# Gate and up biases over 128 rows, down biases in one product at the end

## Chip, core and metric

The kernel runs on one core of one Trainium2 chip. The metric is the device time of one execution in microseconds (us), the median of several runs.

## The reference

A network of two parts works on 512 tokens of width D = 1024 in float32: a first block with a mixed attention and a mixture of experts, then two layers of a second block. The change touches the mixture of experts alone, whose core is:

```
logits = h @ w_router + b_router            # [512, 32]
topv, idx = lax.top_k(logits, 4)
gates = softmax(topv)
# for each expert e and its tokens x:
gu = x @ w_gate_up[e] + b_gate_up[e]        # 1024 -> 2 * 1024
gate = minimum(gu[:, :1024], 7)
up = clip(gu[:, 1024:], -7, 7)
act = (up + 1) * (gate * sigmoid(1.702 * gate))
y = act @ w_down[e] + b_down[e]             # 1024 -> 1024
out[token] += y * gate_of_token
```

and its result is added to the residual x.

## The kernel before

**Accuracy.** A product is near float32 because each operand is held as a value rounded to float32r and the remainder. `split` makes them: ACT writes the rounded tile (`whi`, L50), DVE the remainder (`wlo`, L51). `mm3` then issues three products per tile of weights, L61 with `wlo`, L62 and L63 with `whi`.

**One expert.** Its tokens stand in 96 slots. The weights come in 12 tiles [128, 4, 512] of 1 MB, eight for gate and up and four for down, each loaded by SP into one of eight raw buffers (`fetch`, L85), split by ACT and DVE into four buffers each of `whi` and `wlo`, and used by four groups of three products with 512 columns: 144 products in all. `prep` transposes the gathered rows (L864) and splits them (`exh`, `exl`). `gate_up(e, h)` takes one half of the features: products into two banks G, then the activation with ACT L881 and L882 and DVE L885 to L888, transposed (L891) and split into `ath` and `atl`. `down(e, h)` multiplies a half of the activations into the two banks Y, opened at h = 0; after h = 1 ACT copies the banks, scaled with the gate, into `y` (L912, two buffers), and POOL adds the rows in DRAM by an indirect DMA (`scatter`, L980).

**Biases.** `add_bias` (L846) opens every bank: one product (L848) whose weights are one column of `esel`, broadcast over the 96 slots, over 64 rows, and whose moving operand is 64 rows of the tile `bias`: 32 experts rounded, and 32 remainders. Rows 0 to 63 hold chunks 0 to 2 of 512 columns, rows 64 to 127 chunks 3 to 5; chunks 0 to 3 are gate and up, 4 and 5 down. That is six products per expert, 192 in all, and the tile is made once in `moe_setup` (L810, L812).

**Slots.** `place(e)` finds an expert's tokens and gates: POOL compares (L763), PE multiplies with the one-hot tile (L774 for tokens, L779 for gates), DVE copies (L775, L781, L782). `gather` (L786) fetches the rows. These run up to three experts ahead.

**Order.** The loop over 32 experts issues gate_up(e, 0), prep(e+1), gather(e+2), place(e+3), down(e-1, 1), gate_up(e, 1), down(e, 0). A scheduler in the framework decides how these interleave on each engine; each engine then runs its own list in order. The last expert's result isn't scattered: `yh` and `yl` stay on chip and are added to the loaded sums `xr` in `last(i)` for each of four token tiles, by products with the one-hot tile `pt` (L974) and a DVE addition (L975).

Of the kernel before, what the change touches and what calls it, by code (L numbers as in the profile page):

```python
# [28 lines left out]
# slots of an expert's list in the main path  # L29
NS = 96  # L30
# weight tiles of the experts that are loaded ahead of the router
# [7 lines left out]
class Kern:  # L39
# [6 lines left out]
    def split(self, hi, lo, src, scale=None, eng=None):  # L46
        """hi = src rounded to float32r, lo = src - hi (exact)."""
# [8 lines left out]
    def mm3(self, out, pairs, start=True, stop=True):  # L56
        """out += sum over pairs ((ah, al), (bh, bl)) of a.T @ b in float32 accuracy."""
# [7 lines left out]
    def rstd(self, pool, ss, n, scale, name):  # L65
        """1 / sqrt(ss * scale + EPS): a first value from the exponent's bits and two Newton steps,
        their constants set for the smallest largest error (5e-7)."""
# [21 lines left out]
    def weight(self, src, nk, ncol, pools=None, q=None, parts=1, plan=()):  # L89
        """src: AP [nk*128, ncol] in DRAM. Returns per k tile (hi, lo) APs [128, ncol].  # L90
        plan: for the first chunks, the pools, what the split is to come behind, and the engine of the remainders."""
# [4 lines left out]
        for k0 in range(0, nk, q):  # L96
# [10 lines left out]
            if early:  # L107
                # behind the router's work on each engine
# [15 lines left out]
    def bcast(self, ap, n):  # L124
        """DRAM vector [n] on all partitions."""
        return bass.AP(tensor=ap.tensor, offset=ap.offset, ap=[[0, 128], [1, n]])

    def norm_T(self, i, x, gain, xh, xl, pool, keep=None):
        """Tile i of x [128, D], token-major -> x * rstd * gain, transposed and split."""
# [18 lines left out]
    def setup(self, ctx):  # L148
# [17 lines left out]
        # reversal of the rows  # L166
        rev = self.rev = c.tile([128, 128], F32R, name="rev")
        # diagonal tiles of the second block: a query's own chunk and the earlier ones are open
# [4 lines left out]
    def bias_tables(self, pool):  # L173
        """Bias tables of the banded attention, reversed and extended, over the scale of the scores, split:
        R[m] = 8 * tab[min(639 - m, 256)]"""
# [16 lines left out]
    def probs(self, banks, nh, nk, scale, m, s, normal=False):  # L192
        """banks: scores in psum, [128, nh, nk * 128] each. Leaves the maxima in m and the sums of the exponentials
        in s ([128, heads]); returns per pair of heads and key tile the exponentials, over their sums if normal,
        transposed: (hi, lo) rhs [128, 2 heads, 128]."""
# [34 lines left out]
    def values(self, vs, pr, dst):  # L230
        """Sum over key tiles of values.T @ probs for a pair of heads -> dst [128 (head, dim), 128], whole or (hi, lo)."""
# [10 lines left out]
    def rope_tables(self, pool, cosap, sinap, gain, nrot, name):  # L242
        """A = C * gain, B = Sg * gain with its halves swapped; cos/sin given for the first nrot dims."""
# [18 lines left out]
    def headnorm(self, ps, nh, A, B, nrot, out, i):  # L262
        """ps: psum [128, nh*64] -> per-head rmsnorm and rotation, into out [128, nh, 64]."""
# [3 lines left out]
        # copied, so that the bank is free early  # L267
# [29 lines left out]
    def block1(self):  # L297
# [37 lines left out]
        # fillers after each query tile of the groups and of the dense branch  # L335
# [3 lines left out]
        def bank():  # L339
            """A psum bank of either pool, in turn."""  # L340
            turn[0] += 1
            pool, tag = (self.psS, "S") if turn[0] % 2 else (self.psM, "M")
            return pool.tile([128, 512], F32, name=tag, tag=tag)

        def filler(n=1):
            """Feature tiles of the gates, as tanh(z / 2) = 2 sigmoid(z) - 1, kept in DRAM until the merge."""
# [16 lines left out]
        # masks over key tiles (earlier, own, later): 0 where allowed, NEG elsewhere;  # L363
        # it[p, c] = c - p, key - query = c - p + 128 * rel
# [18 lines left out]
        # keys, transposed and zero-padded: [pair, head of the pair, key]  # L383
# [34 lines left out]
        def scores(qh, ql, p, v, s, j0, j1, mk):  # L418
            """Scores of head s of query pair p, key pair v over key tiles j0..j1."""
# [8 lines left out]
        def scores_b(qh, ql, p, s):  # L428
            """The same for the dense branch; both halves of the partitions hold the keys."""
# [1083 lines left out]
```

## Time and profile before

| | us |
|---|---|
| median of three runs | 3157.68 |
| the three runs | 3156.82, 3157.68, 3165.53 |
| span of the profiled execution | 3154.3 |
| TensorE busy in the span | 3020.5 |
| VectorE busy | 2233.5 |
| ScalarE busy | 1712.6 |

The span runs from the first to the last instruction of one profiled execution. The experts take about 668 to 1936 us of it. Busy times are sums over stages with different limits, so the parts of the experts' stage are read apart, and within them the starts of single instructions. A row of a timeline is: start, duration, engine, line, operation, output<-inputs, shapes, count, and in brackets how long the engine was idle before it and what it waited for. PEld is TensorE's weight load.

### The profile page before, as it was taken

Reading aid. Unit: us, or ns where it says so; the run is one execution under the profiler, and the core shown is the slowest. Engines: PE = TensorE matmul, PEld = TensorE weight load, DVE = VectorE, ACT = ScalarE, POOL = GpSimd, SP = SyncE. Lnnn points to the kernel's source line nnn. Section 1 sums busy time; section 2 is a strip of 40 time slices with the busy share of each in tenths; the row PEclk is TensorE's granted clock in tenths of the full one; section 3 lists DMA queues with packets and bytes.
Section 4 is the critical chain, followed back from the end, with each engine's and each line's share of the span. In section 5 each row is a group of like instructions: output and inputs, shape, how many; then the busy total and the mean of one; then the engine's idle time right before and its main releaser. Section 6 shows DMA issues by size and latency. Waiting matters only on the chain. (4 is left out here: it accounts for less than half of the span.)

```text
span 3154.3 us, 40478 instructions
## 1 busy us (share of the span) xinstructions
PE 3020.5 (96%) x14662; PEld 2327.0 (74%) x14662; DVE 2233.5 (71%) x3715; ACT 1712.6 (54%) x2535; POOL 629.4 (20%) x438
## 2 busy tenths in 40 slices
PE   8999899979999999999999998999999979999998
PEld 6898777766666666666666665878887868888876
DVE  7766587668888988888888987644455585545564
ACT  4645554336776777777777774434444234444432
POOL 1000011033324444444444002111101010111000
PEclk9999999979999999999999998999999989999999
DMA  5122232569999999999999995433435433334362
GB/s 160 61 62 68 88 105 77 181 228 321 350 347 328 338 344 343 343 346 344 343 340 350 344 346 155 128 112 104 122 111 191 150 104 118 113 114 116 102 235 91
DMA packets 407761, 648.48 MB, mean 206 GB/s; under 512 B 23028, under 2 KB 150532, under 8 KB 407556
## 3 DMA queue, kind: packets, MB, share of 16 engines
q1 hardware_dynamic: 387808, 585.73, 55.6%
q0 software_dynamic: 19168, 58.00, 6.1%
q8 instruction: 118, 1.93, 0.3%
q10 hardware_dynamic: 576, 2.10, 0.2%
q14 instruction: 91, 0.71, 0.1%
HBM read 596.16 MB, written 53.79 MB: 206 GB/s over the span
## 5 line engine op out<-in xcount | busy, mean ns | idle before, releaser
L51 DVE TENSOR_TENSOR wlo<-raw,whi 128x2048 fp32r<-128x2048 f32 (+3 forms) x636 | 1157.7, 1831 | 318.6 <-ACT whi L50 314.3
L50 ACT ACTIVATE whi<-raw 128x2048 fp32r<-128x2048 f32 (+3 forms) x646 | 973.2, 1531 | 211.0 <-PE M L63 104.1
L61 PE MATMUL G<-wlo,exh 128*96 128x512 f32 x1024 | 412.8, 403 | 1.8 <-DVE wlo L51 1.8
L63 PE MATMUL G<-whi,exh 128*96 128x512 f32 x1024 | 404.0, 394 | 0.0
L62 PE MATMUL G<-whi,exl 128*96 128x512 f32 x1024 | 403.8, 394 | 0.0
L763 POOL TENSOR_SCALAR poh<-i,rk 128x96 fp32r<-128x96 f32 x124 | 314.4, 2545 | 94.1 <-PE T L779 94.0
L61 PE MATMUL F<-xl,whi 128*128 128x512 f32 x768 | 311.3, 405 | 14.5 <-DVE fl L1199 7.0
L62 PE MATMUL F<-xh,wlo 128*128 128x512 f32 x768 | 304.5, 396 | 1.8 <-DVE wlo L51 1.8
L63 PE MATMUL F<-xh,whi 128*128 128x512 f32 x768 | 304.6, 397 | 0.0
L61 PE MATMUL M<-wlo,xh 128*128 128x512 f32 (+2 forms) x736 | 277.5, 379 | 7.0 <-DVE wlo L51 2.0
L62 PE MATMUL M<-whi,xl 128*128 128x512 f32 (+2 forms) x736 | 276.9, 377 | 0.7 <-DVE xl L51 0.7
L63 PE MATMUL M<-whi,xh 128*128 128x512 f32 (+2 forms) x736 | 273.3, 373 | 0.0
L61 PEld LDWEIGHTS G<-wlo,exh 128*96 128x96 f32 x1024 | 165.5, 162 | 81.2 <-issue 18.2
L63 PEld LDWEIGHTS G<-whi,exh 128*96 128x96 f32 x1024 | 165.5, 162 | 70.4
L62 PEld LDWEIGHTS G<-whi,exl 128*96 128x96 f32 x1024 | 165.9, 162 | 64.2 <-issue 1.2
L61 PE MATMUL Y<-wlo,ath 128*96 128x512 f32 x512 | 210.2, 411 | 2.6 <-POOL wlo L51 1.9
L62 PE MATMUL Y<-whi,atl 128*96 128x512 f32 x512 | 202.1, 395 | 0.0
L63 PE MATMUL Y<-whi,ath 128*96 128x512 f32 x512 | 201.6, 394 | 0.0
L61 PEld LDWEIGHTS F<-xl,whi 128*128 128x128 f32 x768 | 145.3, 189 | 53.4 <-DVE fl L1199 11.2
L61 PEld LDWEIGHTS M<-wlo,xh 128*128 128x128 f32 x736 | 164.7, 224 | 26.3 <-ACT kk L269 4.4
L62 PEld LDWEIGHTS M<-whi,xl 128*128 128x128 f32 x736 | 164.8, 224 | 15.5 <-DVE xl L51 1.4
L63 PEld LDWEIGHTS M<-whi,xh 128*128 128x128 f32 x736 | 164.6, 224 | 14.2 <-issue 0.2
(480 smaller groups left out, 5413.7 us busy)
## 6 DMA issues: line engine op xcount, KB each, us to landing
raw<-in_w_gate_up SPq DMA_DIRECT2D x256, 1024.0 KB, 6.4
raw<-in_w_down SPq DMA_DIRECT2D x124, 1024.0 KB, 7.1
raw<-in_w_in SPq DMA_DIRECT2D x154, 512.0 KB, 3.9
GZ<-fl POOLq DMA_DIRECT2D x80, 256.0 KB, 2.3
raw<-in_w_out SPq DMA_DIRECT2D x24, 512.0 KB, 4.0
raw<-in_w_branch SPq DMA_DIRECT2D x24, 512.0 KB, 4.4
gt<-GZ SPq DMA_DIRECT2D x48, 256.0 KB, 3.1
raw<-in_w_in SPq DMA_DIRECT2D x32, 256.0 KB, 2.9
```

The source lines that it names most:

```text
L50: self.last_act = nc.scalar.activation(hi, src, AF.Copy)
L51: self.last_dve = (eng or nc.vector).tensor_sub(lo, src, f(hi))
L61: nc.tensor.matmul(out, lhsT=ah, rhs=bl, start=start and i == 0, stop=False)
L62: nc.tensor.matmul(out, lhsT=al, rhs=bh, start=False, stop=False)
L63: self.last_mm = nc.tensor.matmul(out, lhsT=ah, rhs=bh, start=False, stop=stop and i == n - 1)
L763: eng.tensor_scalar(oh[:, i], self.i128[:, :NS], self.rk[:, i, e:e + 1], None, op0=ALU.is_equal)
```

## The change

1. `bias` shrinks from [128, 1536] to [128, 1024] and holds only gate and up: rows 0 to 63 chunks 0 and 1, rows 64 to 127 chunks 2 and 3. `esel` becomes [128, 2, 32] with zeros where the other half's rows are, so `add_bias` multiplies all 128 rows.
2. `down` adds no bias; its first product opens the bank. `y` has one buffer, not two.
3. `gates_T`, called once at expert 28, loads b_down three times into 96 rows (a raw buffer), rounds it (`bdn`: rounded, rounded, remainder), copies the gates of all tokens as 96 columns (rounded, remainder, rounded), and transposes them into `gT` [96, 512].
4. `last` opens each bank with a product of `gT` and `bdn`, that is the sum over experts of gate times bias, for all experts at once.
5. The branch for lists over 96 slots (not taken in the trace) drops its addition of b_down. Comments and docstrings are removed, and the lines behind are shifted (L912 becomes L910, L974 becomes L996, L980 becomes L1002).

```diff
-        n = 3 * FF // 2
-        bias = self.bias = mc.tile([128, n], F32R, name="bias")
-        bt = self.mraw.tile([128, 2048], F32, name="bt", tag="raw")[:, :n]
+        bias = self.bias = mc.tile([128, FF], F32R, name="bias")
+        bt = self.mraw.tile([128, 2048], F32, name="bt", tag="raw")[:, :FF]
         for r in (0, 32):
-            nc.sync.dma_start(bt[r:r + 32], a["b_gate_up"][:, :n])
-            nc.sync.dma_start(bt[64 + r:96 + r, :FF // 2], a["b_gate_up"][:, n:])
-            nc.sync.dma_start(bt[64 + r:96 + r, FF // 2:], a["b_down"])
+            nc.sync.dma_start(bt[r:r + 32], a["b_gate_up"][:, :FF])
+            nc.sync.dma_start(bt[64 + r:96 + r], a["b_gate_up"][:, FF:])
...
-        esel = self.esel = mc.tile([128, 32], F32R, name="esel")
+        esel = self.esel = mc.tile([128, 2, 32], F32R, name="esel")
+        nc.gpsimd.memset(f(esel), 0.0)
         for r in range(0, 128, 32):
-            nc.vector.tensor_copy(esel[r:r + 32], self.ident[r:r + 32, r:r + 32])
+            nc.vector.tensor_copy(esel[r:r + 32, r // 64], self.ident[r:r + 32, r:r + 32])
...
         def add_bias(ps, e, c):
-            r = slice(c // 3 * 64, c // 3 * 64 + 64)
-            nc.tensor.matmul(ps, lhsT=esel[r, e:e + 1].to_broadcast([64, NS]), rhs=bias[r, c % 3 * 512:c % 3 * 512 + 512],
-                             start=True, stop=False)
+            nc.tensor.matmul(ps, lhsT=esel[:, c // 2, e:e + 1].to_broadcast([128, NS]),
+                             rhs=bias[:, c % 2 * 512:c % 2 * 512 + 512], start=True, stop=False)
...
-                if h == 0:
-                    add_bias(yp[e][c], e, 4 + c)
-                self.mm3(yp[e][c], [((th[:, k], tl[:, k]), W[k]) for k in range(4)], start=False, stop=h == 1)
+                self.mm3(yp[e][c], [((th[:, k], tl[:, k]), W[k]) for k in range(4)], start=h == 0, stop=h == 1)
             if h == 1 and e < E - 1:
-                y = mp.tile([NS, D], F32, name="y")
+                y = mp.tile([NS, D], F32, name="y", bufs=1)
...
+        gT, bdn = lp.tile([96, S], F32R, name="gT"), lp.tile([96, D], F32R, name="bdn")
+
+        def gates_T():
+            raw = self.mraw.tile([128, 2048], F32, name="bt", tag="raw")
+            bt = raw[:96, :D]
+            for r in (0, 32, 64):
+                nc.sync.dma_start(bt[r:r + 32], a["b_down"])
+            nc.scalar.activation(bdn, bt, AF.Copy)
+            nc.vector.tensor_sub(bdn[64:], bt[64:], f(bdn)[64:])
+            g = raw[:, D:D + NT * 96].rearrange("p (t a e) -> p t a e", t=NT, a=3)
+            for n, c in enumerate((0, 1, 0)):
+                nc.gpsimd.tensor_copy(g[:, :, n], f(self.VG)[:, :, :, c])
+            p = psT.tile([128, 512], F32, name="T", tag="T")[:96]
+            for i in range(NT):
+                nc.tensor.transpose(p[:, i * 128:i * 128 + 128], g[:, i].rearrange("p a e -> p (a e)"), self.ident)
+            nc.scalar.activation(gT, p, AF.Copy)
...
+            if e == E - 4:
+                gates_T()
...
                 ps = self.mbank()
+                ts = slice(i * 128, i * 128 + 128)
+
+                nc.tensor.matmul(ps, lhsT=gT[:, ts], rhs=bdn[:, cs], start=True, stop=False)
                 for n, y in enumerate((yl, yh)):
-                    nc.tensor.matmul(ps, lhsT=pt[:, i * 128:i * 128 + 128], rhs=y[c], start=n == 0, stop=n == 1)
+                    nc.tensor.matmul(ps, lhsT=pt[:, ts], rhs=y[c], start=False, stop=n == 1)
                 nc.vector.tensor_add(xs[i][:, cs], xs[i][:, cs], ps)
```

TensorE (PE), a late expert, around the transposes of the next expert's rows (T from `xg`) and the slot product L774. Before:

```order
L62 MATMUL G<-whi,exl 96x512
L63 MATMUL G<-whi,exh 96x512
L864 MATMUL T<-ident,xg_6279 128x96 x4
L774 MATMUL T<-V,poh 96x2 x4
L848 MATMUL Y<-bias,esel 96x512
L61 MATMUL G<-wlo,exh 96x512
L62 MATMUL G<-whi,exl 96x512
```

After:

```order
L62 MATMUL G<-whi,exl 96x512
L63 MATMUL G<-whi,exh 96x512
L864 MATMUL T<-ident,xg_6280 128x96 x4
L774 MATMUL T<-V,poh 96x2 x4
L61 MATMUL G<-wlo,exh 96x512
L62 MATMUL G<-whi,exl 96x512
L63 MATMUL G<-whi,exh 96x512
```

The product that opened a bank Y is gone from this place, and the dense products of G close up.

VectorE (DVE), a late expert, around the gate copy L781, which waits for PE's L779, and the remainders L51 of weight tiles. Before:

```order
L51 TENSOR_TENSOR wlo<-raw,whi 128x2048 x2
L775 TENSOR_SCALAR gi<-T,spare 96x1
L51 TENSOR_TENSOR exl<-T,exh 128x384
L51 TENSOR_TENSOR wlo<-raw,whi 128x2048
L886 TENSOR_SCALAR gm<-G 96x512
L781 COPY g_12077<-T 96x2
L887 SCALAR_TENSOR_TENSOR sg<-sg,gm 96x512
L782 TENSOR_TENSOR gate<-g_12077 96x1
L51 TENSOR_TENSOR wlo<-raw,whi 128x2048
L885 TENSOR_SCALAR up<-G 96x512
L51 TENSOR_TENSOR wlo<-raw,whi 128x2048
```

After:

```order
L51 TENSOR_TENSOR wlo<-raw,whi 128x2048
L775 TENSOR_SCALAR gi<-T,spare 96x1
L51 TENSOR_TENSOR wlo<-raw,whi 128x2048
L886 TENSOR_SCALAR gm<-G 96x512
L51 TENSOR_TENSOR exl<-T,exh 128x384
L781 COPY g_12351<-T 96x2
L887 SCALAR_TENSOR_TENSOR sg<-sg,gm 96x512
L51 TENSOR_TENSOR wlo<-raw,whi 128x2048
L782 TENSOR_TENSOR gate<-g_12351 96x1
L885 TENSOR_SCALAR up<-G 96x512
L51 TENSOR_TENSOR wlo<-raw,whi 128x2048
```

L782 now stands behind a remainder, one of the remainders ahead of `gi` (L775) is gone from its pair, and `exl` comes between `gm` and the gate copy.

ScalarE (ACT), one expert near the end of the loop, after the change: the copy of `gates_T` (L926) in its surroundings.

```order
L53 ACTIVATE ath<-T 128x384
L50 ACTIVATE whi<-raw 128x2048 x2
L881 ACTIVATE sg<-G,c_6301 96x512
L926 ACTIVATE bdn<-bt 96x1024
L882 ACTIVATE sg<-sg,c_6301 96x512
L50 ACTIVATE whi<-raw 128x2048 x3
L910 ACTIVATE y<-Y,gate 96x512
L50 ACTIVATE whi<-raw 128x2048
```

The copy of b_down has come between the two steps of an activation, L881 and L882.

## Rows read from the trace of the kernel before

**Rows 1.** The page: span of the profiled execution.

```profile
span 3154.3 us, 40478 instructions
```

**Rows 2.** Stretches: us; busy of PE, PEld, DVE, ACT, POOL; PEclk; DMA share; GB/s.

```profile
736.00:966.00 230.00, 230.00 (x1051) 153.75 (x1050) 203.03 (x164) 167.89 (x132) 67.32 (x37) 1.00 1.00 347
1004.00:1892.00 888.00, 887.91 (x3991) 591.90 (x3990) 788.14 (x625) 637.43 (x506) 318.76 (x121) 1.00 1.00 344
```

**Rows 3.** Timeline of PE around one bias product, 936 to 938 us.

```profile
936.07 0.39 PE L62 MATMUL Y<-whi,atl 128*96 128x512 f32 x1
936.30 0.39 PE L63 MATMUL Y<-whi,ath 128*96 128x512 f32 x1
936.62 0.46 PE L848 MATMUL G<-bias,esel 64*96 64x512 f32 x1
937.01 0.47 PE L61 MATMUL Y<-wlo,ath 128*96 128x512 f32 x1
937.32 0.39 PE L62 MATMUL Y<-whi,atl 128*96 128x512 f32 x1
```

**Rows 4.** Timeline of PE around two bias products that coincide.

```profile
904.25 0.39 PE L63 MATMUL G<-whi,exh 128*96 128x512 f32 x1
904.57 0.47 PE L848 MATMUL Y<-bias,esel 64*96 64x512 f32 x1
904.57 0.47 PE L848 MATMUL G<-bias,esel 64*96 64x512 f32 x1
...
905.29 0.39 PE L62 MATMUL G<-whi,exl 128*96 128x512 f32 x1
```

**Rows 5.** Timeline of PE's weight loads around one bias product.

```profile
1907.16 0.15 PEld L848 LDWEIGHTS Y<-bias,esel 64*96 64x96 f32 x1 [0.38 <-issue]
1907.56 0.16 PEld L61 LDWEIGHTS G<-wlo,exh 128*96 128x96 f32 x1 [0.24 <-issue]
1907.64 0.16 PEld L62 LDWEIGHTS G<-whi,exl 128*96 128x96 f32 x1
```

**Rows 6.** Tile bias, by form: duration ns min/median/max, first and last start us.

```profile
L848 PE MATMUL G<-bias,esel x128: 463/470/739, 668.6 to 1885.5; 64*96 64x512 f32 x128
...
L848 PE MATMUL Y<-bias,esel x64: 463/470/738, 689.3 to 1907.2; 64*96 64x512 f32 x64
```

**Rows 7.** The scatter, L980, in 780:950 and 1400:1565 us: duration ns min/median/max.

```profile
L980 POOL DMA_INDIRECT X<-y,gi x5: 1922/1952/1958, 788.4 to 941.0; - x5
...
L980 POOL DMA_INDIRECT X<-y,gi x5: 2265/2292/2295, 1405.1 to 1559.6; - x5
...
DMA to landing us min/median/max: 8.6/8.8/9.9
```

**Rows 8.** Timelines of PE and then DVE, 1491 to 1495 us.

```profile
1491.19 0.42 PE L779 MATMUL T<-VG,poh 128*96 128x2 f32 x4
...
1494.79 0.47 PE L61 MATMUL Y<-wlo,ath 128*96 128x512 f32 x1
...
1491.65 0.15 DVE L781 COPY g<-T 96x2 f32<-96x2 f32 x1 [1.42 <-PE T L779]
1491.73 0.69 DVE L887 SCALAR_TENSOR_TENSOR sg<-sg,gm 96x512 f32<-96x512 f32 x1
...
1492.41 2.28 DVE L51 TENSOR_TENSOR wlo<-raw,whi 128x2048 fp32r<-128x2048 f32 x1
```

**Rows 9.** SP's longest wait, 900 to 1300 us; and one stretch, columns as above.

```profile
SPq L85 <- DVE wlo L51: 314.6, 112, 4.6
...
1420.00:1430.00 10.00, 10.00 (x46) 6.77 (x45) 9.15 (x7) 4.34 (x5) 7.10 (x4) 1.00 1.05 388
```

**Rows 10.** Timeline of the additions behind the experts, 1937 to 1940 us.

```profile
1937.14 0.63 PE L974 MATMUL M<-yl,pt 96*128 96x512 f32 x1
...
1937.57 0.63 PE L974 MATMUL M<-yh,pt 96*128 96x512 f32 x1
...
1939.08 1.06 ACT L133 ACTIVATE xn<-xr 128x1024 f32<-128x1024 f32 x1 [9.60 <-DVE xr L975]
```

More of the change, by code (lines that the diff above doesn't have):

```diff
@@ L1070, in overflow @@
                                 rows(ps, aT, a["w_down"], c * 512)
-                                biased(y[:, c * 512:c * 512 + 512], ps, a["b_down"], c * 512)
-                            nc.vector.tensor_scalar(y, y, gate, None, op0=ALU.mult)
+                                nc.vector.tensor_scalar(y[:, c * 512:c * 512 + 512], ps, gate, None, op0=ALU.mult)
                             self.scatter(y, gi[:, 0:1])
```

## The prediction

> **What bounds the kernel now.** I read the profile in this order: the span, the table of engines by stretch, then the timeline of TensorE (PE) around the products that the change touches, and last the other engines' rows at the one place where PE is closely followed. The span is 3154.3 us [rows 1], the three timed runs have a median of 3157.68 us, so that a run is the span and 3.4 us around it; the sum below is made against the span and added to the median. In both stretches of the experts' stage that are shown, PE is busy in all of the time at full granted clock, DVE in 88 to 89% and ACT in 72 to 73% [rows 2]. There an instruction that PE no longer needs shortens the program, as long as the weight tiles still come in time. The reader should not stop at "PE busy": a busy PE can still run at a poor pitch. So look at the starts: two dense products start 0.23 us apart [rows 3]; I use 0.231, since 144 of them make 33.3 us of an expert. Around a bias product of 64 rows this breaks: product to bias 0.32, bias to next product 0.39, and that one to the one after it 0.31 [rows 3]. From 936.30 to 937.32 us it takes 1.02 us where two pitches are 0.46, so **one bias product costs 0.56 us**, not 0.231. The weight load shows why: it starts late around this product, with PE's loader idle for 0.38 and then 0.24 us on nothing but issue [rows 5]; for the dense product behind it there is none. Two bias products on different halves of the partitions start at the same time, and the pair costs 1.04 less 0.46, 0.58 us [rows 4].
>
> The program has 192 of them, 128 for gate and up and 64 for down [rows 6]. An expert is one scatter: five lie 152.6 us from first to last early, 38.15 each, and 154.5 us late, 38.6 each [rows 7]. In the early pattern one pair of the six products coincides (five costs), later none does (six). The check of this reading: 33.3 + 6 x 0.56 = 36.6, which leaves 2.0 us for the 24 small transposes and slot products of an expert, 0.08 each; with five costs 38.1 comes out, as measured. So the whole period is explained by PE.
>
> **The change part by part.** *Gate and up biases over 128 rows.* Their product becomes like a dense one in rows, columns and type. No row shows one of 128 rows with a broadcast operand: the bounds are 0.231 us (a dense product) and 0.56 (what it is now). I take 0.231, because what sets the 64-row product apart from its neighbours in the rows is its height alone: weights and columns have the same sizes and types.
>
> *Down biases.* 64 products go. *Both together*, per expert: early 5 x 0.56 - 4 x 0.231 = 1.88 us, for 230/38.15 = 6.0 experts, 11.3 us. Late 6 x 0.56 - 0.92 = 2.44 us for (1892 - 966)/38.6 = 24.0 experts, 58.6 us. I count nothing for the first two experts, where PE waits for its inputs.
>
> A rule on this very product stands in the Trainium skill. Its page TensorE: Matmul & The Clock Gate, section "Why this matters for your kernels", says that a single product over 32 rows takes as long as one over 128, and that products on distinct row groups run at the same time. The second half speaks against the change, which gives up the pair that coincides; the trace agrees with it (0.58 us for two), but that is still more than two dense pitches. The trace contradicts its first half: 0.56 us against 0.23.
>
> *What is late next.* With 1.9 to 2.4 us less per expert on PE, the weight tiles must come sooner. The closest follower: PE's gate product L779 at 1491.19 releases DVE's copy L781 at 1491.65, behind which L887 (1491.73) and the remainder of a weight tile (1492.41, 2.28 us long) are queued; PE's first Y product starts 1494.79, 0.10 us after that tile is done [rows 8]. From L779 to Y the chain is 3.50 us and PE's window 3.60. In the changed order the bias product in this window costs 0.33 less and the window is 3.35 where L779 keeps its place: PE waits 0.15 us. The changed order alternates two patterns and one has more products in the window, but the pull on all other tiles grows too. I take twice the worked figure, 0.3 us per expert, 7.2 in the late 24, nothing early; bounds 0 and 1.0. DVE is busy 788.14/888 x 38.6 = 34.3 us per expert [rows 2], which is 94% of the new 36.5: the bound behind PE, not reached.
>
> *Loads.* SP issues a load when a raw buffer is free: in 900 to 1300 us it waited 112 times for DVE's remainder, 314.6 us in all [rows 9]. Faster work issues them sooner. The rate now is 344 to 347 GB/s [rows 2]; with 38.6 to 36.5 us it becomes 364, and 10 us of the trace ran at 388 [rows 9]. Cost 0 here, the other case is a rival.
>
> *gates_T, once.* Four PE transposes, 4 x 0.08 = 0.3 us. ACT two copies, 1.06 us by a copy of 128x1024 [rows 10] and about 0.7; DVE 1.1, half of the 2.28 for 2048 columns. They stand in the queues between work on weight tiles. Its buffer takes one of eight raw slots for a while, worth at most one load's wait, 314.6/112 = 2.8 us. Between 0.3 and 3.5 I take 1.5, since most of this is spread over tiles with a lead. *One y buffer:* ACT's next copy waits for the scatter. That is 2.3 us on POOL and up to 9.9 to landing [rows 7], 12 of the 36 us until the next one; the two copies of an expert are two tiles of twelve apart, 6 us, so it costs nothing. If the landing took over 25 us, ACT would stop, and with it the tiles behind.
>
> *The end.* The eight products L994 precede those of L974, which run 0.43 us from one to the next, against 0.23 elsewhere [rows 10]. All eight cost 3.4 us; the first token tile, which ACT awaits at 1939.08 after 9.60 us [rows 10], has two of them, 0.86. I take 1.0. The last expert's tiles end on loads and splits rather than on PE; where these aren't ahead, part of what the expert before gained is given back: another 1.0, bounds 0 and 2.4 (one expert's gain). The setup is smaller and lies where the early biases wait: 0.
>
> **Sum:** 11.3 + 58.6 - 7.2 - 1.5 - 1.0 - 1.0 = 59.2 us; 3157.7 - 59.2 = 3098.5.
>
> **Rivals.** *1, the height is not the cause* (the broadcast operand, or the change of operands, is): the widened product still costs 0.56. Then only removal counts: 0.56 x 6 early and 1.12 x 24 late, 30.2 us, less 3.5 for the one-offs, 3131. For it: no 128-row broadcast is in the trace. Against: the loader's idle time stands at the 64-row product alone. *1b*: the gap belongs to the place, so that the product is worth 0.231 like every other, and 64 of them give 14.8 less 3.5: 3146. That is the time by the first half of the rule of the Trainium skill above; the 0.56 us speaks against it.
>
> *2, the loads set the pace.* An expert moves 344 x 38.6 = 13.3 MB. For it: DMA's share reads 1.00 [rows 2]. Against: it also reads 1.05 at 388 [rows 9], so it is no ceiling. At 347 GB/s nothing early and 0.3 us late would be left, 3153; a quarter of the way from there to 388, 357, it is 37.2 us: 1.4 x 24 + 0.95 x 6 - 3.5 = 36, 3122. The Trainium skill, DMA: Bandwidth & Descriptors, section "Specifications", gives a limit of about 358 GB/s per core, which would be this case; its section "Bandwidth" has more for a core that runs alone, as here, and the 388 agrees with that.
>
> *3, DVE follows worse:* 1.0 us of stall per late expert instead of 0.3, 3115. For it: DVE at 94%.
>
> *4, slower:* DVE's own stalls stay or grow. Now it idles 38.6 - 34.3 = 4.3 us per expert, 1.42 of it at L781 for L779 [rows 8]. In the changed order L781 has only one remainder less ahead of it at times, so DVE may come there earlier and stand longer, with the tiles queued behind. If the idle time stayed 4.3, only the early gain less one-offs would be left, 3150; from 4.6 on it is slower than before, and at 5.0 by 0.3%: 24 x 0.72 - 7.8 = 9.5, 3167. Against: when DVE comes early, the tiles have a lead.
>
> **How the numbers follow.** About 0.3% (9.5 us) is what a measurement of this kernel can tell from no change. Forecast 0.72, with its own range of 3088 (no stall, no one-offs) to 3108; rival 1 0.06, 1b 0.01, 2 0.08 (0.01 of it within 0.3%), 3 0.09, 4 0.04 (0.015 slower, the rest the same). Faster 0.95, same 0.035, slower 0.015. The range of 8 in 10 takes in rival 3 and most of 2: 3086 to 3126; rival 1 and the rest, some 0.13, are outside.
>
> **What would show it.** Bias products only on G, 128, their neighbours at 0.23 us and no idle loader; a period of 36.2 to 36.5 us between scatters; about 365 GB/s; DVE at 94%; PE waits of some tenths of a us on DVE's wlo per expert. Wrong would make it: 0.32 and 0.39 around the widened product (rival 1), SP's loads landing later and ACT waiting for them (2), DVE idle over 3 us per expert with PE waiting (3, 4).

## The result

The changed kernel takes 3114.76 us (median of four runs, 3111.58 to 3115.71) against 3157.25 us: a ratio of 0.9863 with an interval of 0.9846 to 0.9880. It is 1.4% or 42.5 us faster, clear of noise. The forecast was 59 us; the time lies within the range of 3086 to 3126, but above the forecast's own 3088 to 3108. The page of the kernel after gives the span, to be read against [rows 1]:

```profile
span 3113.9 us, 40384 instructions
```

In the experts' stage PE is still busy almost throughout, DVE is at 91 to 92.5% and the loads come in faster. The view is that of [rows 2], of the kernel after:

```profile
736.00:966.00 230.00, 230.00 (x1092) 163.75 (x1091) 210.32 (x171) 174.01 (x138) 80.97 (x41) 1.00 1.01 353
1004.00:1714.00 710.00, 705.59 (x3314) 493.87 (x3313) 656.60 (x519) 529.96 (x425) 394.95 (x114) 1.00 1.04 359
```

The widened product behaves as a dense one. Here is the timeline of PE around one, and of its weight loads, to be read against [rows 3, 5]:

```profile
775.48 0.39 PE L63 MATMUL Y<-whi,ath 128*96 128x512 f32 x1
775.71 0.39 PE L848 MATMUL G<-bias,esel 128*96 128x512 f32 x1
775.94 0.40 PE L61 MATMUL G<-wlo,exh 128*96 128x512 f32 x1
...
775.49 0.16 PEld L848 LDWEIGHTS G<-bias,esel 128*96 128x96 f32 x1
775.71 0.16 PEld L61 LDWEIGHTS G<-wlo,exh 128*96 128x96 f32 x1
```

The starts lie 0.23 us apart on both sides, and the loader is no longer idle. There are 128 such products and no others on the tile (the view of [rows 6]):

```profile
L848 PE MATMUL G<-bias,esel x128: 390/397/721, 673.7 to 1839.3; 128*96 128x512 f32 x128
```

The pace of the experts is read from the scatter, now L1002, as in [rows 7]. First four of the early ones (duration in ns, first and last start), then three of the late ones in POOL's timeline:

```profile
L1002 POOL DMA_INDIRECT X<-y,gi x4: 2252/2274/2285, 794.9 to 903.7; - x4
...
1419.00 2.22 POOL L1002 DMA_INDIRECT X<-y,gi  x1 [15.98 <-ACT y L910]
1456.55 2.53 POOL L1002 DMA_INDIRECT X<-y,gi  x1 [11.59 <-ACT y L910]
1492.79 2.22 POOL L1002 DMA_INDIRECT X<-y,gi  x1 [15.97 <-ACT y L910]
```

Early an expert takes 36.27 us, which is what the sum of PE's instructions gave (33.3 + 4 x 0.231 + 2.0 = 36.2). Late two take 73.79 us, 36.9 each (they alternate between 37.5 and 36.2): 0.6 us more than the early period, in which PE waits for nothing.

**Where the time went.** The table is worked out from the starts of a few instructions in every profile: when ACT rounds the bias tile, from there to the first dense product of G (L61; bias products stand before it), and to the first scatter; from the first scatter to the 31st; from that to DVE's first addition to `xr`, from there to its last, and on to the end. "Early" and "late" are mean periods of the first 5 and of the 9th to the 26th. All in us. The two rows "again" are e5 and e10 below, the rows behind the first four are the other experiments.

| kernel | rounding | to G | to scatter 1 | scatter 1 to 31 | early | late | to addition 1 | additions | rest | span |
|---|---|---|---|---|---|---|---|---|---|---|
| before | 618.7 | 71.7 | 131.6 | 1154.3 | 38.15 | 38.62 | 32.8 | 16.5 | 1200.4 | 3154.3 |
| before, again | 624.6 | 71.1 | 131.0 | 1154.3 | 38.15 | 38.62 | 32.8 | 16.5 | 1196.7 | 3155.8 |
| after | 625.0 | 75.2 | 133.6 | 1102.3 | 36.28 | 36.87 | 37.2 | 19.5 | 1196.3 | 3113.9 |
| after, again | 625.4 | 74.6 | 131.6 | 1102.3 | 36.28 | 36.87 | 37.1 | 18.9 | 1198.9 | 3114.3 |
| e1 wide only | 626.1 | 71.3 | 131.1 | 1128.3 | 37.48 | 37.71 | 32.6 | 16.4 | 1194.5 | 3129.0 |
| e2 narrow, end | 623.1 | 76.6 | 135.0 | 1130.9 | 37.59 | 37.75 | 37.8 | 19.6 | 1199.3 | 3145.7 |
| e3 no G bias | 622.2 | 67.6 | 133.6 | 1092.2 | 35.57 | 36.58 | 38.1 | 19.1 | 1197.9 | 3103.1 |
| e4 slots | 625.0 | 74.7 | 133.8 | 1091.9 | 36.32 | 36.41 | 33.9 | 18.3 | 1201.0 | 3103.9 |
| e6 96 rows | 620.5 | 76.3 | 134.7 | 1102.3 | 36.30 | 36.87 | 37.3 | 19.5 | 1196.0 | 3110.3 |
| e7 no end | 626.1 | 74.6 | 131.6 | 1100.7 | 36.27 | 36.87 | 36.2 | 16.9 | 1202.2 | 3113.7 |
| e8 no lock | 623.5 | 65.1 | 127.3 | 1102.2 | 36.27 | 36.86 | 31.7 | 19.3 | 1200.9 | 3104.9 |
| e9 slots, no lock | 621.5 | 66.7 | 130.0 | 1092.1 | 36.32 | 36.42 | 26.2 | 18.3 | 1203.3 | 3091.4 |

From the second profile of before to the second of after: rounding +0.8, to the first scatter +0.6, the scatters -52.0, to the first addition +4.3, the additions +2.4, the rest +2.2, in sum -41.7 from these rounded figures (the spans differ by 41.5). The rounding and the rest vary by several us between profiles of one kernel. Of the columns between, the time to the first scatter varies by up to 2.0 us and the others by up to 0.6.

### The profile page after: what moved, and what is told of

The parts are those of the page before. It is cut to its first block, busy times and chain, and to the rows that moved or that the text cites. A ratio compares the mean times of both kernels' runs of the same rounds, so it can differ in the third digit from the quotient of the medians.

```text
span 3113.9 us, 40384 instructions
## 1 busy us (share of the span) xinstructions
PE 2963.8 (95%) x14610; PEld 2326.8 (75%) x14610; DVE 2233.9 (72%) x3716; ACT 1708.7 (55%) x2537; POOL 734.9 (24%) x442
## 5 line engine op out<-in xcount | busy, mean ns | idle before, releaser
L51 DVE TENSOR_TENSOR wlo<-raw,whi 128x2048 fp32r<-128x2048 f32 (+3 forms) x636 | 1162.2, 1838 | 278.4 <-ACT whi L50 273.5
L61 PE MATMUL G<-wlo,exh 128*96 128x512 f32 x1024 | 410.1, 401 | 15.3 <-DVE wlo L51 15.3
L763 POOL TENSOR_SCALAR poh<-i,rk 128x96 fp32r<-128x96 f32 x124 | 378.8, 3066 | 14.6 <-PE T L779 13.6
L61 PE MATMUL F<-xl,whi 128*128 128x512 f32 x768 | 311.6, 406 | 14.6 <-DVE fl L1220 7.0
L61 PE MATMUL M<-wlo,xh 128*128 128x512 f32 (+2 forms) x736 | 277.0, 378 | 7.8 <-DVE wlo L51 2.0
L61 PEld LDWEIGHTS G<-wlo,exh 128*96 128x96 f32 x1024 | 165.8, 162 | 80.7 <-issue 15.9
L61 PE MATMUL Y<-wlo,ath 128*96 128x512 f32 x512 | 207.9, 406 | 12.5 <-POOL wlo L51 6.4
L1223 POOL DMA_DIRECT2D GZ<-fl x80 | 43.7, 546 | 604.1 <-ACT fl L1222 329.2
L61 PEld LDWEIGHTS F<-xl,whi 128*128 128x128 f32 x768 | 145.4, 189 | 53.4 <-DVE fl L1220 11.3
L61 PEld LDWEIGHTS M<-wlo,xh 128*128 128x128 f32 x736 | 164.1, 223 | 27.1 <-ACT kk L269 4.4
L1002 POOL DMA_INDIRECT X<-y,gi x31 | 72.2, 2328 | 472.4 <-ACT y L910 472.4
```

Source lines behind the costliest of these rows:

```text
L51: self.last_dve = (eng or nc.vector).tensor_sub(lo, src, f(hi))
L61: nc.tensor.matmul(out, lhsT=ah, rhs=bl, start=start and i == 0, stop=False)
L763: eng.tensor_scalar(oh[:, i], self.i128[:, :NS], self.rk[:, i, e:e + 1], None, op0=ALU.is_equal)
L1002: self.nc.gpsimd.indirect_dma_start(out=self.X1[:, :], out_offset=bass.IndirectOffsetOnAxis(ap=rows, axis=0), in_=y, in_offset=None, bound ...
L1223: self.st(GZ[l, n], t)
```

## The experiments

**e1, the widening alone.** From the changed kernel (and y has two buffers again, and the first of the two products behind L994 opens the bank):

```diff
+                if h == 0:
+                    r = slice(c * 64, c * 64 + 64)
+                    nc.tensor.matmul(yp[e][c], lhsT=esel[r, c, e:e + 1].to_broadcast([64, NS]), rhs=bias[r, :512],
+                                     start=True, stop=False)
...
-                nc.tensor.matmul(ps, lhsT=gT[:, ts], rhs=bdn[:, cs], start=True, stop=False)
...
-                gates_T()
```

> Of the change only the widening: gate and up biases over 128 rows, and the down product opened by a 64-row product as before (it reads gate and up biases in place of down ones, so the sums are others, the work is the same); nothing at the end. Theory height (a product over 64 rows costs 0.56 us of PE, one over 128 rows 0.231): in the trace the widened products stand 0.23 us from their neighbours and the two on Y still 0.32 and 0.39; 4 x 0.33 = 1.3 us less per expert, about 30 experts, some 5 us given back in waits on DVE: 3157 - 35 = about 3122. Rival (the cost is of the broadcast operand or of the place, not of the rows): the gaps stay and the time is that of before, 3152 to 3160.

It took 3130.24 us, a ratio of 0.9912 (0.9895 to 0.9928). The G products start 0.22 to 0.23 us behind a dense product, and in the early experts the dense product behind them follows 0.23 us later; those on Y have 0.32 to 0.33 and 0.39 to 0.40, unless transposes stand before them. Where a G product follows one on Y, the 0.40 and then 0.31 are those of Y's. The rival falls. The gain is 28 us against the kernel before on the same chip (3158.30), and not 35: the late period fell by 0.91 us where 4 x 0.33 = 1.32 was counted, and the early one by 0.67, since the coinciding pair of [rows 4] is gone and with it 0.56 of saving. In the late experts 0.27 of the missing 0.41 can be seen: two of the first Y products start 0.44 and 0.29 us behind a G bias product instead of 0.23, each 0.05 us after DVE has ended the remainder they need. That is a wait on DVE and not the price of the product.

**e2, the widening undone.**

```diff
-            nc.tensor.matmul(ps, lhsT=esel[:, c // 2, e:e + 1].to_broadcast([128, NS]),
-                             rhs=bias[:, c % 2 * 512:c % 2 * 512 + 512], start=True, stop=False)
+            r = slice(c // 2 * 64, c // 2 * 64 + 64)
+            nc.tensor.matmul(ps, lhsT=esel[r, c // 2, e:e + 1].to_broadcast([64, NS]),
+                             rhs=bias[r, c % 2 * 512:c % 2 * 512 + 512], start=True, stop=False)
```

> The change with its widening undone: gate and up biases over 64 rows as before, the down biases at the end as in the changed kernel. Theory height: 64 products of 0.56 us are gone, of which one per expert was half hidden in the early six: 0.56 x 6 + 1.12 x 24 = 30 us, less 2 for the end and little new waiting: about 3129; 0.32 and 0.39 us around the products that are left. Rival (a removed product gives back a dense pitch of 0.231): 64 x 0.231 - 2 = 13 us, 3144.

It took 3145.34 us, 0.9953 (0.9937 to 0.9970). PE's timeline of this kernel around one bias product (the edit moves L848 to L849):

```profile
812.97 0.39 PE L63 MATMUL Y<-whi,ath 128*96 128x512 f32 x1
813.28 0.46 PE L849 MATMUL G<-bias,esel 64*96 64x512 f32 x1
813.68 0.47 PE L61 MATMUL G<-wlo,exh 128*96 128x512 f32 x1
813.99 0.40 PE L62 MATMUL G<-whi,exl 128*96 128x512 f32 x1
```

The time is near the rival's 3144, yet the rows give it to the theory: the price of 0.56 us is back with the 64 rows, and the early period fell by 0.56 us. The late one fell by 0.87 us for two products, where the theory has 1.12 and the rival 0.46; one first Y product per late expert starts 0.48 to 0.56 us behind its bias product instead of 0.40, 0.05 us after its remainder, which is a part of what is missing there. The rest stands in the other columns of the table: 8 us are lost behind the last scatter (e7 gives 2.0 to 2.6 of them to L994) and 4 before the first, against the second profile of before. Most of that loss is not of the product: the time from the last scatter to the first addition is longer than before in every kernel without the Y products but e8 and e9, and e8 shows why. The time to the first scatter is less certain, since it varies by 2 us.

**e6, 96 rows.** In the changed kernel:

```diff
+            r = slice(0, 96) if c < 2 else slice(0, 128)
-            nc.tensor.matmul(ps, lhsT=esel[:, c // 2, e:e + 1].to_broadcast([128, NS]),
-                             rhs=bias[:, c % 2 * 512:c % 2 * 512 + 512], start=True, stop=False)
+            nc.tensor.matmul(ps, lhsT=esel[r, c // 2, e:e + 1].to_broadcast([r.stop, NS]),
+                             rhs=bias[r, c % 2 * 512:c % 2 * 512 + 512], start=True, stop=False)
```

> The changed kernel with the bias products of the gate half over 96 rows instead of 128 (the rows left out hold zeros), those of the up half as they are. Theory height 64 (what costs is a product that uses half of the rows, next to products that use all): 96 rows run as 128, the neighbours stay 0.23 us away, 3110 to 3119. Rival (every product of another height than its neighbours costs 0.56 us): 0.32 and 0.39 around two products per expert, 0.65 us per expert, 3125 to 3135.

3116.52 us, 0.9872 (0.9854 to 0.9890), and in PE's timeline:

```profile
808.37 0.39 PE L63 MATMUL Y<-whi,ath 128*96 128x512 f32 x1
808.60 0.40 PE L849 MATMUL G<-bias,esel 96*96 96x512 f32 x1
808.83 0.39 PE L61 MATMUL G<-wlo,exh 128*96 128x512 f32 x1
```

A product over 96 rows costs a dense pitch. So it isn't the odd height that costs, but 64 rows among products over 128; 32 were not tried.

**e3, no gate and up bias at all.**

```diff
-                add_bias(p, e, c)
-                self.mm3(p, [((xh[:, k], xl[:, k]), W[k]) for k in range(KT)], start=False)
+                self.mm3(p, [((xh[:, k], xl[:, k]), W[k]) for k in range(KT)])
```

> The changed kernel without its four gate and up bias products per expert (these biases are left out of the result). It takes another 4 x 0.231 = 0.92 us per expert from PE and nothing from DVE or ACT. Theory DVE chain (in the late experts the period is set by DVE, which waits for PE's slot product L774 and then has seven instructions to do before the first Y product's remainder): only the six early experts gain, 5 us, and the late period stays at about 36.8 us: 3109. Rival PE (PE sets the period, its waits are the same few tenths): 30 x 0.92 = 28 us less than the changed kernel, 3087, late period 35.9.

3106.38 us, 0.9840 (0.9824 to 0.9857). Taking 0.92 us per expert from PE shortens the first four periods by all of it (to 35.35 us) and the late ones by 0.29. In this kernel's late experts PE is busy in 831.93 of 846 us, the columns as above:

```profile
1004.00:1850.00 846.00, 831.93 (x3877) 575.41 (x3876) 787.46 (x629) 638.76 (x513) 420.48 (x124) 1.00 1.04 362
```

So something beside PE sets the late period, though not wholly: a third of what PE is spared still arrives there. What sets it is read in the changed kernel. The waits of DVE and PE in 1004 to 1714 us (engine and line, what it waited for: us in all, times, longest), behind them DVE's wait in the kernel before, 1004 to 1750 us:

```profile
DVE gi L775 <- PE T L774: 23.6, 19, 1.3
DVE g L781 <- PE T L779: 2.3, 9, 0.3
...
PE Y L61 <- DVE wlo L51: 4.4, 19, 0.3
```

```profile
DVE g L781 <- PE T L779: 25.5, 18, 1.4
```

The stand of 1.4 us at the gate copy became one of 1.25 us at the token copy, one step earlier in the slots' work. What follows from it, in the timelines of PE and then DVE of the changed kernel:

```profile
1276.83 0.48 PE L774 MATMUL T<-V,poh 128*96 128x2 f32 x4
...
1283.17 0.40 PE L848 MATMUL G<-bias,esel 128*96 128x512 f32 x1
1283.75 0.47 PE L61 MATMUL Y<-wlo,ath 128*96 128x512 f32 x1 [0.18 <-DVE wlo L51]
...
1277.35 0.21 DVE L775 TENSOR_SCALAR gi<-T,spare 96x1 int32<-96x1 f32 x1 [1.25 <-PE T L774]
1277.49 2.28 DVE L51 TENSOR_TENSOR wlo<-raw,whi 128x2048 fp32r<-128x2048 f32 x1
1279.68 0.68 DVE L886 TENSOR_SCALAR gm<-G 96x512 f32<-96x512 f32 x1
1280.29 0.54 DVE L51 TENSOR_TENSOR exl<-T,exh 128x384 fp32r<-128x384 f32 x1
...
1280.82 0.68 DVE L887 SCALAR_TENSOR_TENSOR sg<-sg,gm 96x512 f32<-96x512 f32 x1
1281.42 2.28 DVE L51 TENSOR_TENSOR wlo<-raw,whi 128x2048 fp32r<-128x2048 f32 x1
```

From L774 on DVE works without a gap until the remainder for the first Y product ends at 1283.70. PE has by then done its bias product, and Y starts 0.58 us behind it where 0.23 would do. Then nothing of Y's weights is loaded ahead, and the next start takes 0.31 (1284.06).

**e4, the slots' copies off DVE.** In `slots`, for the experts in the loop:

```diff
+            if act:
+                q = self.small.tile([128, 2], F32, name="g2")
+                nc.scalar.activation(q[:n], p[:, :2], AF.Copy)
+                nc.gpsimd.tensor_scalar(gi[:n], q[:n, 0:1], BASE, self.spare[:n], op0=ALU.add, op1=ALU.min)
+                return
...
+            if act:
+                nc.scalar.activation(g[:n], p[:, 2:], AF.Copy)
+                nc.gpsimd.tensor_add(gate[:n], g[:n, 0:1], g[:n, 1:2])
+                return
```

> The changed kernel with the small copies of the slots (tokens and gates, L775, L781, L782) taken from DVE: ACT copies them out of the bank and POOL does the arithmetic. Theory DVE chain: DVE no longer stands 1.25 us per expert waiting for L774, the remainder for the first Y product has a lead again, the late period falls from 36.85 to 36.3 us: 24 x 0.55 = 13 us less than the changed kernel, 3102. Rival (DVE is short of throughput, or waits for ACT's whi, and L774 only happens to be where it waits; ACT now stands there instead): the late period stays within 0.15 us of 36.85, 3111 to 3118.

3103.41 us, 0.9822 (0.9806 to 0.9838), 11 us better than the changed kernel, 10.4 of them between the scatters. The late period is 36.41 us, 0.1 above the early one, and no wait of PE on DVE is left in 1004 to 1714 us. In this kernel the loads run at 364 GB/s over 846 us (columns as above):

```profile
1004.00:1850.00 846.00, 845.16 (x3984) 595.22 (x3983) 788.71 (x568) 644.65 (x556) 282.54 (x165) 1.00 1.04 364
```

DVE does nearly as much per expert as before, 788.71/846 x 36.41 = 33.9 us. It was not short of time; it stood at the wrong place. The three copies were moved together, so that what each is worth wasn't measured; the wait to be seen stood at the token copy.

**e5, the kernel before again** (no edit).

> The kernel before, a second profile. Up to the biases' rounding on ACT the two kernels run the same work, yet it starts at 618.7 us in the profile of before and at 625.0 after, and at 622 to 626 in the four kernels so far. Theory chance (TensorE's clock falls in other places in each execution): in this profile the rounding starts somewhere between 618 and 626 and not at 618.7 again, with half-clock stretches in the attention at other places. Rival (the change itself moves something there): 618.5 to 619.

The rounding in the two profiles of before, and in the one of after, in ACT's timeline:

```profile
618.68 1.49 ACT L810 ACTIVATE bias<-bt 128x1536 fp32r<-128x1536 f32 x1 [2.71 <-DMA bt<-in_b_down]
```

```profile
624.62 1.49 ACT L810 ACTIVATE bias<-bt 128x1536 fp32r<-128x1536 f32 x1 [3.35 <-DMA r_br<-in_b_router]
```

```profile
624.96 1.06 ACT L809 ACTIVATE bias<-bt 128x1024 fp32r<-128x1024 f32 x1 [2.42 <-DMA bt<-in_b_gate_up]
```

The same kernel differs by 5.9 us there, so that the 6.3 us by which the changed one seemed to start late need no cause in the change. The traces point to the clock: up to the rounding PE's granted clock is 0.50 in 17.0 us of the first profile of before, in 27.2 us of the second and in 30.6 us of the profile of after, in partly other places. 10.2 us more at half the pace would be 5.1 of the 5.9 us, an estimate that takes PE to set the pace there; it isn't the whole account, since the second profile of after has 37.5 us and starts the rounding at 625.4. A comparison of one profile with one would have put them to the change's account.

**e7, no down biases.** In the changed kernel the call of `gates_T` and the eight products L994 are left out (as in e1, without its products on Y).

> The changed kernel without the down biases (no gates_T, no product L994; the sum lacks gates times b_down). By the prediction gates_T and the eight products cost 1.5 and 1.0 us. In the traces the additions at the end last 2.9 us longer with L994, and PE waits 5.5 us in the last expert for a remainder on POOL. Theory port (the wait on POOL comes of the order in which DVE and POOL take turns at the last remainders, set by the faster PE, not by gates_T): the wait stays, about 3 us less than the changed kernel, 3112. Rival (gates_T moved the last tiles): the wait goes too, 3 + 6 us less, 3106.

3110.46 us, 0.9846 (0.9829 to 0.9862), 4 us less than the changed kernel; the times alone don't tell the two apart, the stretches do. The additions take 16.9 us instead of 19.5 (18.9 in the second profile of after), the scatters 1.6 less, the stretch to the first addition 1.0 less, and PE still waits 5.50 us on POOL in the last expert. So gates_T costs 1.6 us, L994 2.0 to 2.6 in the additions and perhaps up to 1.0 ahead of them, and the wait has another cause.

**e8, three remainders taken from POOL.**

```diff
-                pool = len(self.early) in (7, 4)
+                pool = False
...
-        self.nw, self.on_pool = 0, (7, 10, 381, 381.5, 382.5)
+        self.nw, self.on_pool = 0, (10, 381, 381.5)
```

> The changed kernel with three remainders moved from POOL to DVE: the two of the early tiles of the first expert, and the last half tile of the last expert. Theory port (an operation of DVE that reads two tiles of the chip's memory and one of POOL exclude each other, the later one stands until the other or a whole string of the other is done): the first G product starts 60 to 66 us after the biases' rounding instead of 75.2, the first scatter comes some 5 to 9 us earlier against it, PE's wait of 5.50 us on POOL at the last expert falls under 1.5, and the time is 10 to 15 us less than the changed kernel: 3102. Rival (POOL is merely slow on its tiles, or waits for data): DVE gets 2.3 and 1.2 us of work more per tile moved and nothing else changes: 3115 to 3120.

3105.40 us, 0.9835 (0.9816 to 0.9854), 9 us less than the changed kernel, a little under the 10 to 15 expected. First the last expert, in the changed kernel, in the timelines of PE, POOL and DVE, and then POOL and DVE at the same place in the kernel before:

```profile
1881.35 0.74 PE L61 MATMUL Y<-wlo,ath 128*96 128x512 f32 x1 [5.50 <-POOL wlo L51]
...
1869.56 11.74 POOL L51 TENSOR_TENSOR wlo<-raw,whi 128x1024 fp32r<-128x1024 f32 x2
...
1872.88 3.48 DVE L51 TENSOR_TENSOR wlo<-raw,whi 128x1024 fp32r<-128x1024 f32 x3
1876.28 0.54 DVE L54 SCALAR_TENSOR_TENSOR atl<-T,ath 128x384 fp32r<-128x384 f32 x1
1876.75 2.34 DVE L51 TENSOR_TENSOR wlo<-raw,whi 128x1024 fp32r<-128x1024 f32 x2
```

```profile
1913.25 5.20 POOL L51 TENSOR_TENSOR wlo<-raw,whi 128x1024 fp32r<-128x1024 f32 x2
...
1916.89 2.11 DVE L888 SCALAR_TENSOR_TENSOR up<-up,sg 96x512 f32<-96x512 f32 x1
```

Two half tiles took POOL 5.20 us before and 11.74 after. After, DVE's string of remainders runs unhindered until 1879.09 and POOL ends 2.2 us behind it. Before, it was DVE that stood: L888, else 0.69 us, took 2.11 until POOL was done. The work and the tiles are the same; who came first is not. With the last half tile on DVE (e8), the longest wait in PE's products of the last expert is this one:

```profile
PE Y L62 <- DVE atl L54: 0.6, 1, 0.6
```

Behind the wait of 5.50 us the granted clock of PE is 0.50, the lower of its two levels:

```profile
1881.40:1887.00 5.60, 5.60 (x13) 3.67 (x14) 0.00 (x0) 0.00 (x0) 1.62 (x3) 0.50 0.82 263
```

That can't be put down to this wait alone: the clock is also 0.50 at the end of the experts where PE had no such wait, in 1931.5 to 1941.5 us before and in 1878 to 1888 us of e8.

The start of the first expert is the other case. In the changed kernel, PE, DVE and POOL; then DVE and PE with the remainders off POOL:

```profile
700.19 1.14 PE L61 MATMUL G<-wlo,exh 128*96 128x512 f32 x2 [12.93 <-DVE wlo L51]
...
685.99 11.85 DVE L51 TENSOR_TENSOR wlo<-raw,whi 128x2048 fp32r<-128x2048 f32 x1 [3.45 <-ACT whi L50]
...
686.72 8.97 POOL L51 TENSOR_TENSOR wlo<-raw,whi 128x2048 fp32r<-128x2048 f32 x2
```

```profile
682.71 8.96 DVE L51 TENSOR_TENSOR wlo<-raw,whi 128x2048 fp32r<-128x2048 f32 x4 [1.65 <-ACT whi L50]
...
688.51 0.74 PE L61 MATMUL G<-wlo,exh 128*96 128x512 f32 x1 [2.43 <-ACT exh L50]
```

One remainder of 2.28 us took DVE 11.85 while POOL did two; alone, DVE does four in 8.96. The first product of G comes 10 us sooner after the rounding, the first scatter 4 to 6 (5 to 9 were expected), and the last expert is 5.5 us shorter. The theory of the port stands; the rival of a merely slow POOL falls, since it was DVE's own remainder that took 11.85 us.

**e9 and e10, both mends, and the changed kernel again.** e9 joins the edits of e4 and e8.

> Both mends together on the changed kernel: the slots' copies on ACT and POOL, and the three remainders on DVE. If they are independent, as the places of their gains say (late experts for the one, first and last expert for the other), 11 + 9 = 20 us less than the changed kernel: 3095, with a late period of 36.4 us, the first G product 65 us after the biases' rounding and no wait over 1.5 us on POOL in the last expert. Rival (DVE, at 94%, has no room for the remainders once it also follows closely): under 14 us of gain, above 3101.

> The changed kernel, a second profile on the chip of the run above. The stretches that hang on the instructions alone repeat within 0.3 us: early period 36.3, late 36.9, 37.2 us from the last scatter to the first addition; the biases' rounding lies between 620 and 626 us; 3112 to 3118.

e9 took 3090.85 us, 0.9785 (0.9771 to 0.9798) of the kernel before, e10 3117.55 us, 0.9866 (0.9851 to 0.9881). So e9 beats both kernels, the changed one by 26.7 us on the same chip. The late period of 36.42 us and the 66.7 us to the first G product are near what was expected, and PE's longest wait in the products of the last expert is 0.6 us. That is more than the 20 of the sum: the stretch to the first addition came out at 26.2 us, 5.5 shorter than in e8. Most of this can be seen. Behind the last products of Y, PE stands idle before it can finish the first sum of the end: 7.4 us before, 5.2 after, 2.3 in e4, 2.6 and then 4.4 in e8, 2.5 in e9. So in e8 this stand took back 4.4 us of the mend, and in e9 it did not; what sets it is open, the profile names no instruction of work that it waits for. The stretches of e10 repeat as expected, but the one up to the first scatter is 2.0 us shorter and the additions 0.6.

## Why the prediction came out as it did

**Right: what bounds the kernel, and the price.** PE sets the early period wholly and the late one up to 0.59 us of waits, a 64-row product cost 0.56 us and a 128-row one costs 0.23. The early period of 36.27 us is the predicted 36.2, and the saving per early expert 1.87 where 1.88 was worked out. e1, e2 and e6 show that the rows decide, so rivals 1 and 1b fall; with them the rule of the Trainium skill that was weighed (TensorE: Matmul & The Clock Gate, "Why this matters for your kernels"). The Trainium skill has it for 32 rows, which no run here had; between 96 and 128 rows it holds in e6, and among products over 128 rows it doesn't for 64.

**Right: loads and the single y buffer.** 359 GB/s after and 364 in e4 came without a wait of PE on a load in the late experts: rival 2 didn't come about, though the rate passed the per-core limit of about 358 GB/s that the Trainium skill gives (DMA: Bandwidth & Descriptors, "Specifications"). ACT's copies into y wait for PE alone, on the page of waits of the changed kernel:

```profile
ACT y L910 <- PE Y L63: 67.8, 62, 3.3
```

**Mis-sized: the waits on DVE.** Forecast 0.3 us per late expert, bounds 0 and 1.0; measured 36.87 - 36.28 = 0.59. Over 24 experts that is 7 us of the missing 17. The chain was of the predicted kind (slot product, DVE, remainder, first Y product) but had another head: L774 and the token copy, not L779 and the gate copy of [rows 8]. The step kept the wait at its old place although the order around it had changed: in the rows of the order ahead of the prediction, L775 has one remainder less before it, so that DVE comes to it sooner. e4, which takes the three copies off DVE, gives 0.46 of the 0.59 back; so rival 3 was half true, and rival 4 not at all. DVE's share was no ground for either: 94% was forecast, 92.5% measured, and in e4, with nearly the same work in a shorter period, no wait of PE on DVE is left.

**The failed step: the last expert.** Taken at 1.0 with bounds of 0 and 2.4, it cost 4.3. The step weighed loads and splits and left out that POOL makes some of the remainders there, whose half tiles cost PE 5.5 us of waiting (e8). Up to 1.0 of the 4.3 may belong to L994 (e7), and PE's stand ahead of the additions is 2.2 us shorter than before. The steady pattern of [rows 8] doesn't show it; the place where POOL and DVE share the remainders was not among the rows.

**The failed step: the start at no cost.** The first dense product of G came 3.5 us later after the rounding. The changed order puts two POOL remainders back to back against DVE's first. Of the 3.5 us, 0 to 2.6 are left at the first scatter, depending on which of the two profiles of each kernel are compared.

**Mis-sized: the additions.** L994 was put at 1.0 (bounds 0 and 3.4), and cost 2.0 to 2.6 in the additions by e7. PE's timeline after shows why the lower figure was wrong: it counted the first token tile alone, but the products of all tiles stand one behind the other, so that the later additions wait for all before. At the granted clock of 0.50 that PE has in 1894.2 to 1901.0 us, dense products start 0.42 to 0.43 us apart.

```profile
1896.42 0.77 PE L994 MATMUL M<-bdn,gT 96*128 96x512 f32 x1 [5.15 <-DVEq L1010]
1896.99 0.63 PE L996 MATMUL M<-yl,pt 96*128 96x512 f32 x1
1897.41 0.63 PE L996 MATMUL M<-yh,pt 96*128 96x512 f32 x1
```

gates_T was right: 1.5 forecast, 1.6 measured.

**Summed:** the forecast has 11.3 + 58.6 - 7.2 = 62.7 for the experts and 1.5 for gates_T, 61.2 between the scatters; measured 52.0. 7 of the 9 missing us are the waits on DVE. About 2 are PE's own part: from 38.62 us to the 36.28 that PE needs there were 2.34 us to save per late expert, 2.44 were counted, and 24 x 0.10 = 2.4. The last expert and the additions cost 6.7 instead of 2.0, the start up to 2.6 instead of 0. From 59.2 that leaves 42.7 to 45.3; 42.5 was measured by the medians and 41.5 by the second profiles, and the difference is within what the stretches ahead of and behind the experts vary by.

That the time fell into the range of 3086 to 3126 is in part luck. The time is rival 3's 3115, but the stalls are 0.59 of its 1.0 us per late expert, and what filled the rest, the last expert and the start, was outside the bounds given for it: 4.3 against 2.4, up to 2.6 against 0.

## What to carry to other kernels

Read the pitch of an engine that is always busy: 64-row products between 128-row ones cost 0.33 us more than dense ones here, and padding them with zero rows took that away. When the engine in front gets faster, look in the new order for the place where the next engine stands for it, and not at the wait's old place; taking the slots' three small copies, 0.15 to 0.21 us each, out of a busy queue was worth 11 us, a quarter of what the change had gained. Where two engines shut each other out, who comes first can be turned round by a change elsewhere: look at the durations at the start and the end of a stage too, and take a second profile before blaming a shift of a few us on a change.

## What the runs showed of the hardware

DVE and POOL excluded each other for whole instructions, and the one shut out did not get a turn between two back-to-back instructions of the other: 11.85 us for a DVE remainder of 2.28 behind two of POOL, 11.74 us for two POOL half tiles (5.20 before) behind a string of six of DVE. The Trainium skill has the rule (SBUF — State Buffer, "SBUF: two separate sides"): operations of DVE with two inputs in SBUF (the chip's own memory) and those of GpSimd (POOL) that read it hold a shared port exclusively for a whole instruction, whichever starts first, and the other blocks fully. The traces agree, with the prices above. The rule bears on the two terms of the prediction that failed, the last expert and the start.

Among products over 128 rows, one over 96 costs what one over 128 does (0.23 us between starts in e6), one over 64 does not (0.56 us in the kernel before and in e2), and two over different halves start at the same time (904.57 us in [rows 4]).
